# Opposite array quarters for the two heads of a pair in an RWKV-7 chunk recurrence

## The chip, the cores and the metric

The kernel runs on one core of one Trainium2 chip. The metric is device time in microseconds, the median of three runs. TensorE (PE in the profile) multiplies: a weight tile is loaded into its array of 128 rows by 128 columns, and the moving operand streams past it; a product that has only 64 rows (summed over) or only 64 columns (outputs) uses a half of the array, one with 64 of each a quarter, and one with 32 of each a sixteenth. VectorE (DVE), ScalarE (ACT) and GpSimd (POOL) work element by element, SyncE (SP) issues the DMAs. TensorE writes to PSUM banks (512 fp32 values in each of 128 partitions), the other engines move the results on.

## The reference

One layer of a streaming encoder over 256 tokens and 2048 features. The combined projection feeds two groups of heads; their outputs go through one output projection, and a squared-ReLU MLP follows.

```python
h = rms_norm(x, norm_mix); proj = h @ w_in
q_d, k_d, v_d, rw = split(proj)                   # 8 heads of differential attention | RWKV-7
a_out = diff_attention(...)                       # two softmax maps per head: p0 - lam * p1
rw = token_shift(rw, mu); r, kr, vr, lat_w, lat_a, lat_g = split(rw)
w_log  = -softplus(-(w0 + tanh(lat_w) @ w2)) - 0.5; decay = exp(-exp(w_log))
a_rate = sigmoid(a0 + lat_a @ a2);  g = sigmoid(lat_g) @ g2
kk = normalised(kr * k_k); k_mod = kr * (1 + (a_rate - 1) * k_a)
# 16 heads of 64 features, state S (64 x 64) per head, over 256 tokens:
S_t = S_(t-1) diag(w_t) + (S_(t-1) a_t) b_t^T + v_t k_t^T;  y_t = S_t r_t     # a = -kk, b = kk * a_rate
y = (group_norm(y) + bonus) * g
x = x + concat(a_out, y) @ w_out
x = x + square(relu(rms_norm(x) @ mlp_up)) @ mlp_down
```

## The kernel before

The four weight matrices are streamed in tiles of 256 x 512. Each is split exactly into two parts (`hi` by ACT, `lo` by DVE, `split`), and three products per 128 rows and token tile give the result (`gemm`; the products named `acc` in the profile). While the tiles of `w_in` and the first half of `w_out` go by, side work runs beside them: RWKV-7 in two halves of eight heads, then attention in two halves of four heads. A side task is a generator; each `yield dve, act, hop` declares what its next stage costs VectorE and ScalarE and how many weight tiles it waits, and `pump` lets a task go on while the credit of `BD` and `BA` (2.0 us each) per weight tile lasts.

All instructions are first taken down by `Recorder` (so every row of the profile has line 292), then put in order by `plan`: a list scheduler with costs for each instruction. Each engine takes the instruction that can start first, earlier ones before later; weight splits get a rank 120 places ahead (`SPL`). The chip executes each engine's list in that order. Side products share four PSUM banks (tags `sm` and `tr`), weight products have four more.

The recurrence works in chunks of 64 tokens, four per half. For each half of eight heads:

- `seg_kr` makes decay and rate through low-rank products (`lora_mm`): one with both parts of the weights under each other (128 rows), one with the small part of the latents (64 rows, `XL`).
- `seg_b` and `seg_r` write the decayed r, k, a and b into `AR` and `BK`, whose columns hold a chunk pair as [r|k even, a|b even, a|b odd, r|k odd]; the partitions hold the 64 features of two heads, of which the even one has partitions 0 to 63.
- `seg_a` multiplies `BK` and `AR` into the chunk matrices `Am` (64 rows, 128 columns, 128 elements a head; four heads of one row half, then four of the other), masks them, sends the block N of each through DRAM to one block a partition, inverts the diagonal 32-blocks there, and joins them by products of 32x32 (`TP`, `Rm`).
- `seg_c` runs the chunks in turn. The bank `XY` takes `Am` over V (rows of r|k, 128 columns) and the state product `AR` over `Sp`. Its a|b part goes to `X`, `Rm` over `X` gives U (`UV` holds V and U under each other), `tm` over `UV` gives the state (128 rows, 64 columns, heads of a pair in alternate column halves), and `Am` over U is added to the r|k part of `XY`, which becomes `Y`.

All eight heads of a chunk use the same row half in these products: `pk, pb = 64 * e, 64 - 64 * e` with `e = c % 2`. The attention (`seg_attn`) multiplies q and k of the two maps, which lie in the two row halves (64 rows), one map after the other.

After the side work of a half, `finish` lets what is left of its tasks go on, and the output projection multiplies y first and the attention's output second (`gemm([ys[1], as_[1]], ...)`).

## Time and profile before

| | us |
|---|---|
| three runs | 1237.98, 1239.23, 1240.45 (median 1239.23) |
| span of the profiled execution (first to last instruction) | 1236.8 |
| median of the runs over that span | 2.4 |
| PE busy | 1225.0 |
| DVE busy | 842.1 |
| ACT busy | 727.0 |
| POOL busy | 6.7 |
| mean granted TensorE clock | 0.999 |

The profile gives a span for its execution and no time of its own; what a run has around the span is taken from the difference to the median. Busy time of PE counts from the start of a product to the end of its last result, and products overlap; so a block of products is best read from its start to the start of the row behind it.

### The profile page before, as it was taken

To read this page: it belongs to the slowest core of one execution; us is meant where nothing else is said; L and a number is where in the kernel's file an instruction comes from. 1 tells how busy PE (TensorE), PEld (TensorE's weight loads), DVE (VectorE), ACT (ScalarE), POOL (GpSimd) and SP (SyncE) were. 2 spreads that over 40 slices of the span, in tenths; PEclk is the share of its full clock that TensorE was granted. 3 is DMA by queue.
4 is the path that set the end of the run, shared out by engine and by line. 5 is a ranking of instruction groups with operands and counts; after the bars stand their busy time and mean duration, and the time that the engine had idled before them with its cause. 6 is when DMAs were issued, how large, how long until landed. Compare 5 with 4: busy or idle time off the path is not lost.

```text
span 1236.8 us, 16428 instructions
## 1 busy us (share of the span) xinstructions
PE 1225.0 (99%) x6089; PEld 988.9 (80%) x6089; DVE 842.1 (68%) x1257; ACT 727.0 (59%) x1145; POOL 6.7 (1%) x28
## 2 busy tenths in 40 slices
PE   8999999999999999999999999999999999999998
PEld 6878887888778788878788787887887887888786
DVE  5578684697847776777747648658658558567754
ACT  6684455665567667977447447456457356357532
POOL 1000000000000000000000000000000000000000
PEclk9999999999999999999999999999999999999999
DMA  8745646256442645566565665665665665666564
GB/s 256 204 142 158 168 135 179 63 145 171 128 138 90 228 153 167 173 187 204 187 188 181 193 187 178 196 187 174 201 177 181 203 176 184 203 172 199 192 205 135
DMA packets 126560, 216.10 MB, mean 175 GB/s; under 512 B 21584, under 2 KB 24400, under 8 KB 126480
## 3 DMA queue, kind: packets, MB, share of 16 engines
q1 hardware_dynamic: 126480, 215.05, 57.5%
q8 instruction: 48, 0.79, 0.3%
q14 instruction: 32, 0.26, 0.1%
HBM read 211.09 MB, written 3.93 MB: 174 GB/s over the span
## 4 chain that ended last, share of the span: by engine, by line
PE 93%; ACT 3%; DVE 2%; DMA 1%; issue 1%; SPq 0%; ACTq 0%
PE acc L292 83%; PE sm L292 7%; PE tr L292 3%; ACT z L292 1%; DVE z L292 1%; ACT hi L292 1%; DMA x<-x 1%; DVE lo L292 0%; DMA TP<-Td 0%; ACT hT L292 0%; SPq L292 0%; ACT junk L292 0%; DVE hT L292 0%; DVE x L292 0%; DMA Td<-N 0%
## 5 line engine op out<-in xcount | busy, mean ns | idle before, releaser
L292 DVE TENSOR_TENSOR lo<-raw,hi 128x1024 fp32r<-128x1024 f32 (+2 forms) x393 | 474.2, 1210 | 307.0 <-ACT hi L292 303.3
L292 ACT CAST hi<-raw 128x1024 fp32r<-128x1024 f32 (+2 forms) x393 | 405.6, 1038 | 336.9 <-PE acc L292 316.6
L292 PE MATMUL acc<-hi,u 128*128 128x512 f32 x1024 | 324.0, 395 | 2.7 <-DVE z L292 2.7
L292 PE MATMUL acc<-hi,hT 128*128 128x512 f32 x1024 | 322.6, 395 | 0.0
L292 PE MATMUL acc<-hi,xT 128*128 128x512 f32 (+1 forms) x832 | 267.3, 395 | 1.2 <-ACT hi L292 1.2
L292 PEld LDWEIGHTS acc<-hi,u 128*128 128x128 f32 x1024 | 192.8, 188 | 50.5 <-issue 5.5
L292 PEld LDWEIGHTS acc<-hi,hT 128*128 128x128 f32 x1024 | 192.8, 188 | 45.2
L292 PE MATMUL acc<-lo,hT 128*128 128x512 f32 x512 | 202.1, 395 | 0.2 <-DVE lo L292 0.2
L292 PE MATMUL acc<-lo,u 128*128 128x512 f32 x512 | 202.0, 395 | 0.0
L292 PEld LDWEIGHTS acc<-hi,xT 128*128 128x128 f32 x832 | 153.4, 189 | 33.6 <-ACT hi L292 1.7
L292 PE MATMUL acc<-lo,xT 128*128 128x512 f32 (+1 forms) x416 | 163.4, 393 | 0.1
L292 ACT ACTIVATE z<-acc,rstd 32x128 f32<-32x128 f32 x256 | 91.9, 359 | 47.2 <-DVE z L292 27.3
L292 PEld LDWEIGHTS acc<-lo,hT 128*128 128x128 f32 x512 | 96.4, 188 | 23.1 <-DVE lo L292 0.6
L292 PEld LDWEIGHTS acc<-lo,u 128*128 128x128 f32 x512 | 96.4, 188 | 22.2
L292 DVE TENSOR_SCALAR z<-acc,rstd 32x128 f32<-32x128 f32 x256 | 90.2, 352 | 18.6 <-ACT z L292 14.9
L292 PEld LDWEIGHTS acc<-lo,xT 128*128 128x128 f32 x416 | 78.4, 189 | 16.0 <-DVE lo L292 1.0
L292 DVE TENSOR_TENSOR x<-x,acc 128x512 f32<-128x512 f32 x80 | 52.0, 680 | 5.6 <-PE acc L292 5.4
L292 PE MATMUL acc<-hi,y 128*128 128x512 f32 x128 | 42.7, 400 | 0.0
L292 PE MATMUL acc<-hi,a 128*128 128x512 f32 x128 | 42.1, 398 | 0.0
L292 ACT ACTIVATE uf<-uf 128x1024 f32<-128x1024 f32 x16 | 17.0, 1062 | 35.8 <-DVE uf L292 35.8
L292 PEld LDWEIGHTS acc<-hi,a 128*128 128x128 f32 x128 | 24.0, 188 | 5.9 <-issue 0.3
L292 PEld LDWEIGHTS acc<-hi,y 128*128 128x128 f32 x128 | 23.9, 189 | 5.5 <-issue 0.3
(228 smaller groups left out, 850.3 us busy)
## 6 DMA issues: line engine op xcount, KB each, us to landing
raw<-up SPq DMA_DIRECT2D x128, 512.0 KB, 3.8
raw<-down SPq DMA_DIRECT2D x128, 512.0 KB, 3.8
raw<-w_in SPq DMA_DIRECT2D x95, 512.0 KB, 3.7
raw<-w_out SPq DMA_DIRECT2D x32, 512.0 KB, 3.7
raw<-w_in SPq DMA_DIRECT2D x8, 288.0 KB, 2.9
x<-x SPq DMA_DIRECT2D x4, 512.0 KB, 6.5
out<-x SPq DMA_DIRECT2D x8, 256.0 KB, 3.4
x<-x SPq DMA_DIRECT2D x6, 256.0 KB, 7.9
```

The costliest lines, as they stand in the source:

```text
L292: op.fn(*op.args, **op.kw)
```

## The change

The two heads of a pair take opposite halves of the rows: with `first(c, q)` the r|k part of head q in chunk c stands at partition 64 * ((c + q) % 2). `AR` and `BK` are written by partition half with the columns ordered accordingly, `UV` and `Y` are copied in two column sets (`hcols`). In `seg_c` the state product comes first; then `Am` over V makes only the a|b part, with 64 columns, the two heads of a pair in opposite quarters of the array, as in the product with `Rm`. The output's r|k part is one product of `Am` over V and U (128 rows, 64 columns) behind the state. In `seg_a` and `seg_attn` the products of the two row halves are issued alternately into two banks, and the products of the inverses alternate between the two 64-row halves. In `lora_mm` the second product has 128 rows too, with zeros in the half that was left out (`XWL`, `XAL`); `lam_p` moves to a shared slot to make room for them. Declared costs of stages change with the copies. Comments and docstrings go. The core of the diff:

```diff
-    XW, XA, XL, G0, G0L, G1 = (cst.tile([P, T], F32R, name=n) for n in ("XW", "XA", "XL", "G0", "G0L", "G1"))
+    XW, XA, XWL, XAL, G0, G0L, G1 = (cst.tile([P, T], F32R, name=n) for n in ("XW", "XA", "XWL", "XAL", "G0", "G0L", "G1"))
+    nc.gpsimd.memset(XWL[64:128].bitcast(F32), 0.0)
+    nc.gpsimd.memset(XAL[0:64].bitcast(F32), 0.0)
...
-        nc.vector.tensor_sub(XL[0:64], lw, XW[0:64])
-        nc.vector.tensor_sub(XL[64:128], la, XA[64:128])
+        nc.vector.tensor_sub(XWL[0:64], lw, XW[0:64])
+        nc.vector.tensor_sub(XAL[64:128], la, XA[64:128])
...
-    def ab(X):
-        return X.rearrange("p (a x) -> p a x", x=256)[:, :, 64:192].rearrange("p a (e t) -> p a e t", e=2)
-    def kr_(X):
-        return X.rearrange("p (a g t) -> p a g t", g=4, t=64)[:, :, 0:4:3, :]
-    def g4(X):
-        return X.rearrange("p (a e) t -> p a e t", e=2)
-    def f4(X):
-        return X.rearrange("p f (c e t) -> p (f c) e t", c=2, e=2)
+    def rows(q):
+        return slice(64 * q, 64 * q + 64)
+    def quarter(X, q, inner):
+        v = X[rows(q)].rearrange("p (a g t) -> p a g t", g=4, t=64)
+        return v[:, :, 1:3, :] if inner else v[:, :, 0:4:3, :]
+    def ab(X, q):
+        return quarter(X, q, q == 0)
+    def kr_(X, q):
+        return quarter(X, q, q == 1)
+    def g4(X, q):
+        return X[rows(q)].rearrange("p (a e) t -> p a e t", e=2)
+    def f4(X, q):
+        return X[rows(q)].rearrange("p f (c e t) -> p (f c) e t", c=2, e=2)
+    def first(c, q):
+        return 64 * ((c + q) % 2)
+    def hcols(X, q):
+        return X.rearrange("p (f q i) -> p q f i", q=2, i=64)[:, q]
...
-    def lora_mm(Dx, X, rows, out, bias):
+    def lora_mm(Dx, X, XL, out, bias):
         for fp in range(2):
             b = bank("tr")
             for i in range(2):
                 f = 2 * fp + i
                 nc.tensor.matmul(b[:, i * T:(i + 1) * T], Dx[:, f * P:(f + 1) * P], X, start=True, stop=False)
-                nc.tensor.matmul(b[:, i * T:(i + 1) * T], Dx[rows, f * P:(f + 1) * P], XL[rows], start=False, stop=True)
+                nc.tensor.matmul(b[:, i * T:(i + 1) * T], Dx[:, f * P:(f + 1) * P], XL, start=False, stop=True)
...
-        yield 1.1, 0.0, 0
+        yield 2.2, 0.0, 0
         AR, BK = big("AR"), big("BK")
         H.AR, H.BK = AR, BK
-        nc.vector.tensor_mul(ab(AR), f4(kk), g4(G[:, :, 0:64]))
-        done()
-        yield 1.1, 0.0, 0
-        nc.vector.scalar_tensor_tensor(ab(BK), f4(tau), -0.5, g4(Gi), op0=ALU.mult, op1=ALU.mult)
-        done()
-        yield 1.1, 0.0, 0
-        nc.vector.tensor_mul(kr_(BK), f4(km), g4(Gi))
+        for q in range(2):
+            nc.vector.tensor_mul(ab(AR, q), f4(kk, q), g4(G[:, :, 0:64], q))
+        done()
+        yield 2.2, 0.0, 0
+        for q in range(2):
+            for e in range(2):
+                nc.vector.scalar_tensor_tensor(ab(BK, q)[:, :, e], f4(tau, q)[:, :, e], -0.5, g4(Gi, q)[:, :, e], op0=ALU.mult, op1=ALU.mult)
+        done()
+        yield 2.2, 0.0, 0
+        for q in range(2):
+            nc.vector.tensor_mul(kr_(BK, q), f4(km, q), g4(Gi, q))
...
-        yield 1.1, 0.0, 0
-        nc.vector.tensor_mul(kr_(H.AR), f4(r), g4(H.G[:, :, 1:]))
+        yield 2.2, 0.0, 0
+        for q in range(2):
+            nc.vector.tensor_mul(kr_(H.AR, q), f4(r, q), g4(H.G[:, :, 1:], q))
...
-            nc.scalar.copy(H.UV[0:64, 2 * t, :], b[0:64])
-            nc.scalar.copy(H.UV[64:128, 2 * t + 1, :], b[64:128])
+            for e in range(2):
+                for q in range(2):
+                    o = first(e, q)
+                    nc.scalar.copy(hcols(H.UV[o:o + 64, 2 * t + e, :], q), hcols(b[64 * e:64 * e + 64], q))
...
         for c in range(4):
-            e = c % 2
-            pb = 64 - 64 * e
             Am = ftile([P, 8, P], "Am")
             H.Am.append(Am)
-            for q in range(2):
-                yield 0.6, 0.0, 0
-                b = bank("sm")
-                rows = slice(64 * q, 64 * q + 64)
-                for i in range(4):
-                    cs = i * 512 + c * P
-                    nc.tensor.matmul(b[:, i * P:(i + 1) * P], H.BK[rows, cs:cs + P], H.AR[rows, cs:cs + P], start=True, stop=True)
-                nc.vector.tensor_mul(Am[:, 4 * q:4 * q + 4, :], b.rearrange("p (h t) -> p h t", h=4),
-                                     masks[:, e:e + 1, :].broadcast_to([P, 4, P]))
-            nc.sync.dma_start(Ndv[e, c // 2], Am[pb:pb + 64, :, pb:pb + 64])
+            yield 1.2, 0.0, 0
+            bs = [bank("sm") for _ in range(2)]
+            for i in range(4):
+                cs = i * 512 + c * P
+                for q in range(2):
+                    nc.tensor.matmul(bs[q][:, i * P:(i + 1) * P], H.BK[rows(q), cs:cs + P], H.AR[rows(q), cs:cs + P], start=True, stop=True)
+            for q, b in enumerate(bs):
+                e = (c + q) % 2
+                pb = 64 - first(c, q)
+                hs = slice(4 * q, 4 * q + 4)
+                nc.vector.tensor_mul(Am[:, hs, :], b.rearrange("p (h t) -> p h t", h=4), masks[:, e:e + 1, :].broadcast_to([P, 4, P]))
+                nc.sync.dma_start(Ndv[e, c // 2][:, hs], Am[pb:pb + 64, hs, pb:pb + 64])
...
+        yield 0.0, 1.0, 0
+        bvs = [bank("sm").rearrange("p (c h t) -> p c h t", c=2, h=8) for _ in range(2)]
+        for c2 in range(2):
+            for h in range(8):
+                for e in range(2):
+                    pb = 64 - 64 * e
+                    nc.tensor.matmul(bvs[e][pb + 32:pb + 64, c2, h, :], H.Am[2 * c2 + (e + h // 4) % 2][pb:pb + 32, h, pb + 32:pb + 64],
+                                     TP[pb:pb + 32, c2, h, :], start=True, stop=True)
         for e in range(2):
             pb = 64 - 64 * e
-            yield 0.0, 0.5, 0
-            b = bank("sm")
-            bv = b.rearrange("p (c h t) -> p c h t", c=2, h=8)
-            for c2 in range(2):
-                Am = H.Am[2 * c2 + e]
-                for h in range(8):
-                    nc.tensor.matmul(bv[pb + 32:pb + 64, c2, h, :], Am[pb:pb + 32, h, pb + 32:pb + 64], TP[pb:pb + 32, c2, h, :],
+            nc.scalar.copy(TP[pb + 32:pb + 64], bvs[e][pb + 32:pb + 64])
+        yield 0.0, 1.0, 1
+        bvs = [bank("sm").rearrange("p (c h t) -> p c h t", c=2, h=8) for _ in range(2)]
+        for c2 in range(2):
+            for h in range(8):
+                for e in range(2):
+                    pb = 64 - 64 * e
+                    nc.tensor.matmul(bvs[e][pb:pb + 32, c2, h, :], TP[pb + 32:pb + 64, c2, h, :], Rm[pb + 32:pb + 64, c2, h, 32:64],
                                      start=True, stop=True)
-            nc.scalar.copy(TP[pb + 32:pb + 64], bv[pb + 32:pb + 64])
-        yield 0.0, 0.0, 1
         for e in range(2):
             pb = 64 - 64 * e
-            yield 0.0, 0.5, 0
-            b = bank("sm")
-            bv = b.rearrange("p (c h t) -> p c h t", c=2, h=8)
-            for c2 in range(2):
-                for h in range(8):
-                    nc.tensor.matmul(bv[pb:pb + 32, c2, h, :], TP[pb + 32:pb + 64, c2, h, :], Rm[pb + 32:pb + 64, c2, h, 32:64],
-                                     start=True, stop=True)
-            nc.scalar.copy(Rm[pb:pb + 32, :, :, 32:64], bv[pb:pb + 32])
+            nc.scalar.copy(Rm[pb:pb + 32, :, :, 32:64], bvs[e][pb:pb + 32])
...
+        heads_ = [(f, q, slice(f * P + 64 * q, f * P + 64 * q + 64)) for f in range(4) for q in range(2)]
         for c in range(4):
-            e = c % 2
-            pk, pb = 64 * e, 64 - 64 * e
             Am = H.Am[c]
-            yield 0.0, 0.5, 1
+            pks = [first(c, q) for q in range(2)]
+            kr_rows, ab_rows = [slice(o, o + 64) for o in pks], [slice(64 - o, 128 - o) for o in pks]
+            yield 0.0, 0.6, 1
             XY = bank("sm")
-            if True:
-                for h in range(8):
-                    cs = slice(h * 64, h * 64 + 64)
-                    nc.tensor.matmul(XY[:, cs], Am[pk:pk + 64, hq(h), :], UV[pk:pk + 64, c, cs], start=(h == 0), stop=True,
-                                     skip_group_check=True)
             if c:
                 for f in range(4):
                     nc.tensor.matmul(XY[:, f * P:(f + 1) * P], H.AR[:, f * 512 + c * P:f * 512 + (c + 1) * P], Sp[:, f, :],
-                                     start=False, stop=True, skip_group_check=True)
+                                     start=(f == 0), stop=True, skip_group_check=True)
+            for f, q, cs in heads_:
+                nc.tensor.matmul(XY[ab_rows[q], cs], Am[kr_rows[q], 4 * q + f, ab_rows[q]], UV[kr_rows[q], c, cs],
+                                 start=(not c and f == 0), stop=True, skip_group_check=True)
             X = stile([P, 512], "X", 1)
-            nc.scalar.copy(X[pb:pb + 64], XY[pb:pb + 64])
-            yield 0.0, 0.5, 1
+            for q in range(2):
+                nc.scalar.copy(hcols(X[ab_rows[q]], q), hcols(XY[ab_rows[q]], q))
+            yield 0.0, 0.6, 1
             Ub = bank("sm")
-            for h in range(8):
-                cs = slice(h * 64, h * 64 + 64)
-                nc.tensor.matmul(Ub[pb:pb + 64, cs], H.Rm[pb:pb + 64, c // 2, hq(h), :], X[pb:pb + 64, cs], start=True, stop=True)
-            nc.scalar.copy(UV[pb:pb + 64, c, :], Ub[pb:pb + 64])
-            yield 0.7, 1.2, 1
+            for f, q, cs in heads_:
+                nc.tensor.matmul(Ub[ab_rows[q], cs], H.Rm[ab_rows[q], c // 2, 4 * q + f, :], X[ab_rows[q], cs], start=True, stop=True)
+            for q in range(2):
+                nc.scalar.copy(hcols(UV[ab_rows[q], c, :], q), hcols(Ub[ab_rows[q]], q))
+            yield 0.7, 1.3, 1
             if c < 3:
                 Sb = bank("sm")
-                for h in range(8):
-                    o = (h // 2) * P + 64 * (h % 2)
-                    nc.tensor.matmul(Sb[64 * (h % 2):64 * (h % 2) + 64, (h // 2) * 64:(h // 2) * 64 + 64],
-                                     H.tm[c][:, o:o + 64], UV[:, c, h * 64:h * 64 + 64], start=True, stop=True)
+                for f, q, cs in heads_:
+                    nc.tensor.matmul(Sb[rows(q), f * 64:f * 64 + 64], H.tm[c][:, cs], UV[:, c, cs], start=True, stop=True)
                 Sbv = Sb[:, :256].rearrange("p (f j) -> p f j", f=4)
                 gc = H.GC[:, :, c:c + 1].broadcast_to([P, 4, 64])
                 if c:
...
                     nc.gpsimd.memset(Sp, 0.0)
                 nc.scalar.copy(Sp[0:64, :, 0:64], S[0:64])
                 nc.scalar.copy(Sp[64:128, :, 64:128], S[64:128])
-            for h in range(8):
-                cs = slice(h * 64, h * 64 + 64)
-                nc.tensor.matmul(XY[pk:pk + 64, cs], Am[pb:pb + 64, hq(h), pk:pk + 64], UV[pb:pb + 64, c, cs], start=False, stop=True,
-                                 skip_group_check=True)
-            nc.scalar.copy(Y[pk:pk + 64, c // 2, :], XY[pk:pk + 64])
+            for f, q, cs in heads_:
+                nc.tensor.matmul(XY[kr_rows[q], cs], Am[:, 4 * q + f, kr_rows[q]], UV[:, c, cs], start=False, stop=True, skip_group_check=True)
+            for q in range(2):
+                o = 64 * (c % 2)
+                nc.scalar.copy(hcols(Y[o:o + 64, c // 2, :], q), hcols(XY[kr_rows[q]], q))
...
-                for m in range(2):
-                    rows = slice(64 * m, 64 * m + 64)
-                    b = bank("sm")
-                    bv = b[:, :2 * nk].rearrange("p (h k) -> p h k", h=2)
-                    for i in range(2):
-                        hd = 2 * hp + i
-                        nc.tensor.matmul(bv[:, i, :], H.q[rows, hd, qt * P:(qt + 1) * P], H.k[rows, hd, :nk], start=True, stop=True)
+                bvs = [bank("sm")[:, :2 * nk].rearrange("p (h k) -> p h k", h=2) for _ in range(2)]
+                for i in range(2):
+                    hd = 2 * hp + i
+                    for m in range(2):
+                        rows = slice(64 * m, 64 * m + 64)
+                        nc.tensor.matmul(bvs[m][:, i, :], H.q[rows, hd, qt * P:(qt + 1) * P], H.k[rows, hd, :nk], start=True, stop=True)
+                for m, bv in enumerate(bvs):
```

## Rows read from the trace of the kernel before

**Rows 1.** The page: busy us, share of the span and instructions of each engine.

```profile
PE 1225.0 (99%) x6089; PEld 988.9 (80%) x6089; DVE 842.1 (68%) x1257; ACT 727.0 (59%) x1145; POOL 6.7 (1%) x28
```

**Rows 2.** What PE waited for from 60 to 470 us: in total, times, longest.

```profile
PE sm L292 <- DMA TP<-Td: 0.5, 1, 0.5
```

**Rows 3.** Two stretches: length, then busy us of PE, PEld, DVE, ACT, POOL.

```profile
60.00:414.00 354.00, 353.38 (x2265) 286.00 (x2265) 257.19 (x455) 217.63 (x354) 0.84 (x2) 1.00 0.49 138
226.00:280.00 54.00, 54.00 (x366) 44.62 (x365) 48.59 (x72) 35.21 (x53) 0.53 (x1) 1.00 0.40 117
```

**Rows 4.** PE's timeline in chunks of the first half: start us, us, instruction.

```profile
210.28 1.14 PE L292 MATMUL sm<-X,Rm 64*64 64x64 f32 x16
211.36 0.50 PE L292 MATMUL acc<-lo,xT 128*128 128x512 f32 x1
213.18 0.69 PE L292 MATMUL sm<-UV,tmbk 128*64 128x64 f32 x16
213.79 1.14 PE L292 MATMUL sm<-UV,Am 64*64 64x64 f32 x16
214.87 0.38 PE L292 MATMUL tr<-con,hss 128*8 128x128 f32 x2
217.32 2.00 PE L292 MATMUL sm<-UV,Am 64*128 64x64 f32 x16
219.13 0.49 PE L292 MATMUL sm<-rb,spread 64*128 64x256 f32 x2
```

**Rows 5.** PE's timeline, chunk matrices of one chunk.

```profile
266.72 1.71 PE L292 MATMUL sm<-AR,BK 64*128 64x128 f32 x16
268.36 0.72 PE L292 MATMUL acc<-hi,xT 128*128 128x512 f32 x2
```

**Rows 6.** PE's timeline, attention scores in two stages.

```profile
308.95 0.72 PE L292 MATMUL sm<-k,q 64*128 64x128 f32 x8
309.60 0.73 PE L292 MATMUL acc<-hi,xT 128*128 128x512 f32 x2
...
319.12 1.13 PE L292 MATMUL sm<-k,q 64*128 64x256 f32 x4
320.18 0.50 PE L292 MATMUL acc<-hi,xT 128*128 128x512 f32 x1
```

**Rows 7.** PE's timeline, low-rank products of the decay, then gate products.

```profile
160.30 0.28 PE L292 MATMUL tr<-XW,DW 128*128 128x256 f32 x1
...
162.69 0.50 PE L292 MATMUL acc<-hi,xT 128*128 128x512 f32 x1
163.03 0.39 PE L292 MATMUL acc<-lo,xT 128*128 128x512 f32 x1
163.26 0.62 PE L292 MATMUL acc<-hi,xT 128*128 128x512 f32 x2
...
248.57 0.28 PE L292 MATMUL sm<-G,gp 128*128 128x256 f32 x1
248.69 0.28 PE L292 MATMUL sm<-G0L,gp 128*128 128x256 f32 x1
```

**Rows 8.** PE's timeline, a block of the inverses.

```profile
200.19 1.17 PE L292 MATMUL sm<-TP,Am 32*32 32x32 f32 x32 [0.48 <-DMA TP<-Td]
201.28 0.50 PE L292 MATMUL acc<-lo,xT 128*128 128x512 f32 x1
```

**Rows 9.** Groups by form, DVE and ACT: shapes, count, busy us, mean ns, idle.

```profile
L292 DVE TENSOR_TENSOR AR<-kk,G 128x1024 f32<-128x1024 f32 x2 | 2.4, 1224 | 0.1
...
L292 ACT COPY Sp<-S 64x256 f32<-64x256 f32 x12 | 4.8, 402 | 3.5 <-DVE S L292 3.3
L292 ACT COPY X<-sm 64x512 f32<-64x512 f32 x8 | 4.6, 579 | 3.6 <-PE sm L292 3.6
```

**Rows 10.** PE's timeline, last transposes of the attention and their first use.

```profile
468.52 1.03 PE L292 MATMUL tr<-con,ao 128*128 128x128 f32 x8
...
473.58 0.40 PE L292 MATMUL acc<-hi,a 128*128 128x512 f32 x1
```

More of the change, by code (lines that the diff above doesn't have):

```diff
@@ L586, in record @@
     nc.vector.tensor_scalar(sub8, pc("sub"), 0.8, None, op0=ALU.mult)
-    lam_p = stile([P, 2, 64], "lam", 1)
+    lam_p = ftile([P, 2, 64], "lam")
     nc.vector.tensor_mul(lam_p, pc("lq").rearrange("p (c d) -> p c d", c=2), pc("lk").rearrange("p (c d) -> p c d", c=2))
@@ L752, in seg_kr @@
         th = ftile([P, 4, T], "th")
-        lora_mm(DW, XW, slice(0, 64), th, [w0h[:, f0 + f:f0 + f + 1] for f in range(4)])
+        lora_mm(DW, XW, XWL, th, [w0h[:, f0 + f:f0 + f + 1] for f in range(4)])
         kr = ftile([P, 4, T], "kr")
@@ L787, in seg_kr @@
         tau = ftile([P, 4, T], "tau")
-        lora_mm(DA, XA, slice(64, 128), tau, [a0h[:, f0 + f:f0 + f + 1] for f in range(4)])
+        lora_mm(DA, XA, XAL, tau, [a0h[:, f0 + f:f0 + f + 1] for f in range(4)])
         yield 1.2, 1.3, 1
```

## Prediction

> **What bounds the kernel now.** I read the page's busy times first: TensorE (PE) is busy 1225.0 of a span of 1236.8 us, VectorE (DVE) 842.1, ScalarE (ACT) 727.0 [rows 1]. A busy share alone could hide waiting, so the next view was the waits of PE between 60 and 470 us, the stretch in which the recurrence and the attention run beside the weight products: PE waited once, for 0.5 us [rows 2]. In that stretch PE therefore goes from one product to the next, and a side product costs the kernel exactly the time by which it pushes the following weight product away. The third view is PE's timeline: the price of a block of side products is the start of the next row less its own start, not its "us" column, which counts the last product's tail as well. The windows say what else is near its limit: from 60 to 414 us DVE is busy 257.2 of 354 us and ACT 217.6, but from 226 to 280 us DVE is busy 48.6 of 54 [rows 3]. An fp32 product stands in the trace as two records (sixteen for the eight heads of a chunk) [rows 4]; blocks are counted in records here.
>
> **The change part by part, savings on PE first.** Eight chunks are run (two halves of heads, four chunks each).
>
> (a) The first product of a chunk, Am over UV, uses 64 rows and 128 columns for eight heads in one row half, all sixteen records behind one another: 1.81 us (217.32 to 219.13) [rows 4]. Afterwards it has 64 columns, and the heads of a pair alternate between opposite quarters. The trace has no such block. Lower bound of its price: the state product, sixteen records alternating between two column halves, 0.61 us (213.18 to 213.79). Upper bound: sixteen records of 64x64 in one quarter, the product with Rm, 1.08 us (210.28 to 211.36) [rows 4]. I take 0.61, since quarters that share neither rows nor columns are further apart than the halves that already overlap. Eight times 1.20 is 9.6 us (at 1.08: 5.8).
>
> (b) The product with Rm goes from one quarter to two opposite ones: 1.08 to 0.61, eight times 0.47, 3.8 us; nothing if the quarters do not overlap.
>
> (c) The second product of the output (64x64, 1.08 us, 213.79 to 214.87) becomes one over 128 rows with 64 columns, in alternating column halves. That is the shape of the state product, so 0.61 is shown: 3.8 us, and up to 4.6 because it follows the state product without a change of shape.
>
> The Trainium skill, page "TensorEngine Tiling (Array Packing)", Restrictions and Gotchas, Gotcha 1, says that different row tiles cannot access the same PSUM bank at once. In (a) and (b) the two heads use different row halves and write the same bank, though different partitions of it; by that rule the twins would take turns, and the sum would be 7.6 us smaller. The rows that overlap here are either one row tile (state product, one bank) or two row tiles with two banks (scores), so the trace does not decide it.
>
> (d) Chunk matrices: sixteen records per chunk, first one row half, then the other: 1.64 us (266.72 to 268.36) [rows 5]. Interleaved twins on two row halves are seen in the scores: eight records in 0.65 us (308.95 to 309.60) [rows 6]. Of that some 0.2 us is the change of shape at entry and exit (a weight product behind a 64-row block takes 0.34 us, 162.69 to 163.03, against 0.23 for the next [rows 7]), so sixteen cost about 1.10. That saves 0.54 for a block that stands alone (4.3 in all), less where two chunks follow each other and overlap at the seam already; with two separate 0.65 it would be 2.7. I take 3.6.
>
> (e) Inverses: blocks of 32 records of 32x32 at 1.09 us (200.19 to 201.28) [rows 8], eight of them, 8.7 us. They become four blocks of 64 with twins in different row groups. Full overlap saves 4.4, none saves 0.3 (fewer changes of shape). By the ratio of (b), 0.61 to 1.08, it is 3.8, which I take.
>
> (f) The low-rank products of decay and rate: eight in 2.39 us (160.30 to 162.69) [rows 7], four such blocks, 9.6 us. Every second one has 64 rows, so the shape changes at each. With zeros in the other rows all have 128, like the gate products that start 0.12 us apart (248.57 to 248.69) [rows 7]: about 1.0 us a block. 5.6 us, and 0.4 for four exits without a change: 6.0 (5.0 to 6.1).
>
> (g) Scores: where both banks were free the twins overlap already (0.65 us for eight); a block in which one bank came late takes 1.06 us for four records (319.12 to 320.18) [rows 6] and is paid twice. Only such stages gain: 1.0 us, between 0 and 2.
>
> (h) Fewer changes of shape in the recurrence, because the first product now stands behind the product with Sp and the output behind the state product: six to eight changes of some 0.11 us, 0.9 (0 to 1.8).
>
> Sum: 9.6 + 3.8 + 3.8 + 3.6 + 3.8 + 6.0 + 1.0 + 0.9 = 32.5 us. With every bound at its bad end 17.6, at its good end 36.6.
>
> **What it adds.** On DVE three products of 128x1024 at 1.22 us become two each of 64 partitions; time goes by the elements of a partition, so each costs twice 1.22; the one with the scalar becomes four of half length, about 2.6 us. That is 5.1 us a half, 10.2 in all. On ACT 32 copies of 64x512 at 0.58 us become 64 of 64x256, at 0.40 by the copies of Sp [rows 9]: 7.0 us. SP issues eight more DMAs for the blocks N (half the size each); weight loads stand behind them in its queue, but they run tiles ahead. All of this is hidden by PE so long as the side work keeps pace with the weight tiles. From 60 to 414 us PE would need about 354 - 31 = 323 us, and DVE 257 + 10 = 267: covered on average. Between 226 and 280 us it is not: the 5.1 us of the second half fall there, PE shortens by two chunks and four matrices (some 6 us), and DVE would need 53.7 us of 48. The order written out beforehand gives the weight splits precedence, so some 6 us of side work slide back rather than PE stopping. What is late next is the attention of the second head group: its output is transposed at 468.52 and first multiplied at 473.58 [rows 10], a margin of 5 us. The chunk's chain also grows, by the first product (0.61) that now waits for Sp and by three split copies (0.22 each), 1.3 us a chunk; weight products cover it. For all this I take back 3 us (0 to 15).
>
> Net 29.5. The profiled span of 1236.8 becomes 1207.3; the median of the runs, 1239.23, lies 2.4 above that span, so the prediction is **1210 us**.
>
> **Rivals.** *Twins in one bank take turns.* This is the rule on banks above as a mechanism of this kernel: in (a) 1.08 instead of 0.61, in (b) nothing. It costs 7.6 us: 1217. For it: no overlapping pair of row halves in the trace shares a bank. Against: the state product's column halves share one and overlap.
>
> *The side work becomes the bound.* DVE's slack between 60 and 414 us falls from 97 to 56 us, and in its full stretches to nothing; if the two joins (before each half of the output projection) each wait for an attention that is 5 to 10 us late beyond the margin, 10 to 17 us are lost in place of 3: 1217 to 1224. For it: the full stretch and the margin of 5 us [rows 3, 10]. Against: the 56 us that are left.
>
> *Slower than before.* A paired stage takes two of the four side banks before it starts. There are twenty such stages (four of matrices, two of inverses, four of scores in each half). PE executes in the written order, so a second bank that is not free holds up the weight products behind it. It decides from 1.5 us a stage (29.5 / 20); at 2 us the kernel takes 1250. Against: PE waits 0.5 us in all now, and the order is planned with the banks in it.
>
> *No new overlap at all.* If interleaving brings nothing, only the shapes gain: (a) 5.8, (c) 3.8, (e) 0.3, (f) 6.0, less 3: 1226.
>
> **How the numbers follow.** Forecast 0.62 (its own range 1203 to 1216), bank rule 0.15, side work 0.15, no overlap 0.03, blocked stages 0.05. About 0.2% (2.5 us) is what a measurement of this kernel can tell from no change. Only blocked stages reach the other side, 0.04 slower and 0.01 within; side work adds 0.01 within: faster 0.94, same 0.02, slower 0.04. The range runs from 1202 (36 us gained, nothing given back) to 1225, which takes in the bank rule and the side work and leaves out most of the last two.
>
> **What would show it.** PE's timeline: sixteen records of the first product, of the product with Rm and of the output in 0.6 us each; matrices 1.1; inverses 64 records in 1.1 to 1.7; low-rank products 0.12 apart. Starts of twins only some ns apart would confirm (a) and (b), an even 0.06 the bank rule. PE's waits between 60 and 470 us should stay below 4 us; waits on weight splits or on the attention's output would show the side work, waits of side products on ACT or DVE the blocked stages. What would make it wrong most: a written order so different that PE waits where nothing waits now.

## The result and the profile after

The changed kernel takes 1224.55 us (median of four runs, 1224.13 to 1227.26) against 1238.61 for the kernel before on the same chip: ratio 0.9893, 95% interval 0.9881 to 0.9906. It is 14 us faster; 29.5 were forecast (1210 us), so less than half of the gain came, and the time lies at the upper end of the range (1202 to 1225). The profiled span is 1222.3 us.

The page, busy us of each engine, answers to [rows 1]:

```profile
PE 1208.6 (99%) x6089; PEld 973.5 (80%) x6089; DVE 848.4 (69%) x1269; ACT 734.9 (60%) x1179; POOL 7.3 (1%) x30
```

PE's timeline (start us, us, instruction), answers to [rows 4], [rows 6] and [rows 8]:

```profile
203.23 1.19 PE L292 MATMUL sm<-TP,Am 32*32 32x32 f32 x32
...
206.76 1.01 PE L292 MATMUL sm<-Rm,TP 32*32 32x32 f32 x27
207.71 0.50 PE L292 MATMUL acc<-lo,xT 128*128 128x512 f32 x1
208.14 1.36 PE L292 MATMUL sm<-Rm,TP 32*32 32x32 f32 x32
209.43 0.47 PE L292 MATMUL sm<-X,Rm 64*64 64x64 f32 x2
209.83 0.79 PE L292 MATMUL acc<-hi,xT 128*128 128x512 f32 x1
210.55 1.11 PE L292 MATMUL sm<-X,Rm 64*64 64x64 f32 x14
...
212.84 1.12 PE L292 MATMUL sm<-UV,tmbk 128*64 128x64 f32 x16
213.75 1.07 PE L292 MATMUL sm<-UV,Am 128*64 128x64 f32 x14
...
217.40 0.68 PE L292 MATMUL sm<-UV,Am 64*64 64x64 f32 x16
218.01 0.50 PE L292 MATMUL sm<-rb,spread 64*128 64x256 f32 x2
...
220.46 0.69 PE L292 MATMUL sm<-UV,tmbk 128*64 128x64 f32 x16
220.98 0.63 PE L292 MATMUL sm<-UV,Am 128*64 128x64 f32 x14
221.93 0.50 PE L292 MATMUL acc<-hi,xT 128*128 128x512 f32 x1 [0.33 <-ACT pvr L292]
...
317.14 1.13 PE L292 MATMUL sm<-k,q 64*128 64x256 f32 x4
318.19 0.50 PE L292 MATMUL acc<-hi,xT 128*128 128x512 f32 x1
...
322.80 1.13 PE L292 MATMUL sm<-k,q 64*128 64x256 f32 x4
323.86 0.50 PE L292 MATMUL acc<-hi,xT 128*128 128x512 f32 x1
```

Three things are to be seen. The first product's sixteen records take 0.61 us (217.40 to 218.01): opposite quarters do overlap. The paired stages often do not run as pairs: two records of the product with Rm run alone, then a weight product, then fourteen; an inverse block stands as 32 records by themselves; the scores of the two maps, four records each, are 5.66 us apart. And between the weight products (`acc`) that start at 209.83 and 221.93 there is no other: a pause of 12.1 us. It ends when ACT has evacuated `pvr`, the second half's last projection. The kernel before had a pause of 7.8 us; the weight products on either side of it:

```profile
212.85 0.40 PE L292 MATMUL acc<-lo,xT 128*128 128x512 f32 x1
...
220.62 0.72 PE L292 MATMUL acc<-hi,xT 128*128 128x512 f32 x2
```

The windows from 200 to 225 us, before and after (length, busy us of PE, PEld, DVE, ACT, POOL, then the granted clock):

```profile
200.00:225.00 25.00, 24.81 (x294) 19.91 (x294) 6.49 (x9) 13.12 (x22) 0.00 (x0) 1.00 0.34 107
```

```profile
200.00:225.00 25.00, 23.79 (x312) 19.13 (x312) 8.18 (x11) 16.33 (x33) 0.00 (x0) 0.86 0.39 108
```

From 208.97 to 215.80 us, for 6.8 us, TensorE's clock is at its lower level, 1.2 GHz; it did not fall there before. The fall begins just ahead of the pause, at the end of the inverses' blocks: 96 records of 32x32 and one weight product from 205.72 to 209.43.

PE's time by kind of product, from each record's start to the next one's, summed over the trace, so that waits behind a record and stretches at the lower clock are in it (the last two columns are kernels of the experiments):

```
us                        before  after  forecast  grouped  grouped + freed load
(a) first product, (c) output  23.84  11.69   10.4    11.45     9.64
(b) product with Rm             8.58   7.88    4.8     7.48     5.29
(d) chunk matrices             12.44  11.33    8.8     9.36     8.47
(e) inverses                    8.96   8.68    5.2     6.58     4.68
(f) low-rank products           9.64   4.59    3.6     4.58     3.91
(g) scores                      8.56  10.55    7.6     6.64     7.04
sum                            72.02  54.72   40.4    46.09    39.03
```

So TensorE saved 17.3 us in these kinds, not 31.6 ((a) to (g) of the forecast), and some 3 us of that went back: the product with Sp takes 0.8 us more than before, the other side products 2.2.

### The profile page after: what moved, and what is told of

It reads as the page before. It is cut to its first block, busy times and chain, and to the rows that moved or that the text cites. A ratio compares the mean times of both kernels' runs of the same rounds, so it can differ in the third digit from the quotient of the medians.

```text
span 1222.3 us, 16497 instructions
## 1 busy us (share of the span) xinstructions
PE 1208.6 (99%) x6089; PEld 973.5 (80%) x6089; DVE 848.4 (69%) x1269; ACT 734.9 (60%) x1179; POOL 7.3 (1%) x30
## 2 busy tenths in 40 slices
DMA packets 126689, 216.11 MB, mean 177 GB/s; under 512 B 21712, under 2 KB 24528, under 8 KB 126608
## 4 chain that ended last, share of the span: by engine, by line
PE 89%; ACT 6%; DVE 2%; issue 1%; DMA 1%; SPq 0%; ACTq 0%
PE acc L292 82%; PE sm L292 5%; PE tr L292 3%; ACT hi L292 1%; ACT z L292 1%; DVE z L292 1%; DMA x<-x 1%; DVE lo L292 1%; ACT UV L292 0%; ACT junk L292 0%; ACT hT L292 0%; SPq L292 0%; DVE hT L292 0%; ACT L292 0%; DVE x L292 0%
## 5 line engine op out<-in xcount | busy, mean ns | idle before, releaser
L292 PEld LDWEIGHTS acc<-hi,y 128*128 128x128 f32 x128 | 23.8, 188 | 5.8 <-issue 0.3
```

What stands on the lines that cost most here:

```text
L292: op.fn(*op.args, **op.kw)
```

## The experiments

Times are medians; each ratio is to the kernel before on the same chip, with its 95% interval.

**Twins kept together (T1), the transfers' queue (T2), VectorE's work (T3).** The order is written by `plan`, which takes whichever product can start first. X, the inverse's operands and the score banks become ready in parts, so it issues one twin before the other.

```diff
...
+    for g in groups.values():          # the products of one paired stage
+        ext = set().union(*(o.deps for o in g)) - set(g)
+        want = list(dict.fromkeys(n for o in g for n in o.tiles))
+        for o in g:
+            o.deps |= ext              # ready together
+            o.want = want              # claim their banks together
...
```

> Every paired stage (first product, product with Rm, state, output, chunk matrices, the two inverse stages, scores) is kept together in the written order: its products become ready together and claim their banks together. Nothing else changes. Theory T1 (the twins were pulled apart by the written order, since their operands and banks become ready at different moments, so that the forecast sum of 32.5 us came out as about 19): the inverse stages overlap their twins (8.7 to 5 us), the product with Rm falls from 7.9 to about 5, scores from 10.6 to about 7, chunk matrices from 11.3 to about 9; the kernel takes 1209 to 1215 us, 10 to 15 below the changed kernel. Theory T3 (the added VectorE and ScalarE work gave the gain back): TensorE's blocks shorten as above, but waits take their place, and the time stays within 3 us of 1224.5. Theory T4 (a stage that needs two banks at once blocks the written order): slower than 1224.5, with TensorE waiting for VectorE or ScalarE.

Measured 1218.52 (0.9844, 0.9831 to 0.9857): 6.0 us better, not 10 to 15. The stages shorten (table, 8.6 us in sum): scores and chunk matrices as T1 says, the inverses to 6.6 us and not 5, the product with Rm to 7.5 and not 5, since its two blocks in the pause take 3.5, at the lower clock or with a wait behind them. T4 falls. The edit joins the twins' operands and their banks at once, so it does not tell which of the two had parted them. But the pause grows:

```profile
202.93 0.39 PE L307 MATMUL acc<-hi,xT 128*128 128x512 f32 x1
...
220.95 0.50 PE L307 MATMUL acc<-hi,xT 128*128 128x512 f32 x1 [0.32 <-ACT pvr L307]
```

TensorE is there 7 us earlier and resumes 1 us earlier: 18.0 us of pause.

```diff
-                nc.sync.dma_start(Ndv[e, c // 2][:, hs], Am[pb:pb + 64, hs, pb:pb + 64])
+                nc.gpsimd.dma_start(Ndv[e, c // 2][:, hs], Am[pb:pb + 64, hs, pb:pb + 64])
```

> The eight transfers a half that take the chunk blocks N to DRAM are issued from GpSimd's queue instead of SyncE's, where they stand between weight loads that wait for buffers. Nothing else changes. Theory T2 (SyncE's in-order queue delays the inverse by some 8 to 10 us a half, the recurrence and the attention are late, bulk products run out of slots near 206 to 222 us and the clock falls to half for 6.8 us): the inverse of the first half starts near 141 us instead of 149, TensorE keeps 2.4 GHz through 206 to 222 us, and the kernel takes 1219 to 1222 us. T1 alone (the delay costs nothing, since weight products cover it): within 1.5 us of 1224.5, the clock falls as before or elsewhere.

Measured 1227.35 (0.9908, 0.9895 to 0.9921): nothing gained. All eight transfers are issued by 129 us instead of 140, and the load of N that follows them still stands at 143.94 in SyncE's queue. T2 as stated falls; what places that load stayed open.

> Both edits: paired stages kept together, and the transfers of N on GpSimd's queue. If T1 and T2 both hold, their gains add: 1205 to 1211 us. If T1 alone: 1209 to 1215, like the grouped kernel. If T2 alone: 1219 to 1222. If T3 (VectorE and ScalarE work is the bound): not below 1221.

Measured 1219.15 (0.9842, 0.9828 to 0.9856), like the grouped kernel.

```diff
+            nc.vector.tensor_mul(ab(AR, q), f4(kk, q), g4(G[:, :, 0:64], q))    # and two more, each a second time
```

> The six half-width VectorE products that the change made out of three (k and a, k and r columns of AR and BK) are executed twice each, with the same values: about 14.6 us more VectorE work in all, half of it in each half of the heads. Theory T3 (the added VectorE and ScalarE work gave the gain back): the kernel takes 5 to 15 us longer than the changed one, 1230 to 1240 us, with TensorE waiting for VectorE or for the late attention. T1 and T2: covered by TensorE, within 2 us of 1224.5.

Measured 1244.85 (1.0053, 1.0039 to 1.0068): 20 us lost, more than the work itself. Of the theories only T3 allows that, though the other way round nothing happens:

```diff
-        for q in range(2):
+        for q in range(1):             # in AR and BK; the second head's half is zero
...
```

> The changed kernel without the VectorE work that it added: of AR and BK only the first head's half is computed (four products a half of heads, as many and as long as before), the second head's half is set to zero by GpSimd, so the recurrence of every second head works on zeros. TensorE executes the same products. T5 with T3 (VectorE is full between 60 and 125 us, so the 5 us added there delay the first half's recurrence, and the end of the pause, one for one): the pause ends 4 to 6 us earlier and the kernel takes 1217 to 1221 us. T1 alone: within 2 us of 1224.5. The added work as the whole cause: 1214 us or less.

Measured 1224.99 (0.9893, 0.9877 to 0.9909): unchanged. In its trace the first half's inverse starts at 149.23 us, as in the changed kernel (149.36), and the pause is longer, 19.8 us, with the clock down for 17.1. So the added VectorE work is not what holds the inverse back; since the pause came out differently, this run does not price that work by itself (the run with N's load freed, below, does it better).

**What the pause waits for (T5), and the clock (T6).** As I read the program, from about 143 us on all 18 working tiles are taken. The evacuation into `pvr` needs one, and gets it when the first half's second chunk is through; with two projections complete in PSUM and neither evacuated, weight products stop. (In the changed kernel with one tile more, below, that evacuation starts at 209.39 us instead of 221.19.) If so, a shorter recurrence ends the pause:

```diff
-        for t in range(31, 0, -1):
+        for t in range(31, 0 if hh else 15, -1):
```

> The grouped kernel with 16 of the 31 steps of the first half's forward substitution on VectorE left out (that half's inverse is incomplete, so its output is not the reference's). TensorE executes the same products; the recurrence's chain of the first half gets shorter by 15 to 20 us. T5: the pause of 18 us falls below 5, the clock stays up there, and the kernel takes 1204 to 1211 us. If the first half's chain is not what sets the pause: within 2 us of 1218.5.

Measured 1209.50 (0.9770, 0.9757 to 0.9783), 9.0 us better than the grouped kernel. The longest stretch without a weight product near 200 us is 3.6, and the clock stays up. The first half's recurrence is what the pause waits for. The steps left out are also 10.4 us less work for VectorE; the freed load of N (below) takes no work from it and gains as much.

```diff
-        t_r = task(seg_r(H, hh, project(3072 + 512 * hh, 512, "pr")), 2, (t_b,))
+        t_r = task(seg_r(H, hh, project(3072 + 512 * hh, 512, "prx" if hh else "pr")), 2, (t_b,))
```

> The changed kernel; only the projected r of the second head half is held in one of the 8 large tiles (one is unused there) and not in one of the 18 working tiles, so one more working tile is free from about 143 us on. Theory T5 (the first half's recurrence is the critical path to 221 us: all 18 working tiles are taken, and the evacuation of the next projection waits until the second chunk frees one; weight products then pause, 212.8 to 220.6 us before, 209.8 to 221.9 after, 202.9 to 220.9 with grouped twins, so TensorE's savings up to there are waited away and the clock falls): the pause of 12.1 us shrinks below 4, the clock stays at 2.4 GHz there, and the kernel takes 1212 to 1219 us. T3 in its plain form (VectorE's and ScalarE's total work is the bound) and T1 alone: within 2 us of 1224.5.

> Both: paired stages kept together and the projected r of the second half in a large tile. T5: the pause of 18 us shrinks below 5, and the gain of grouping shows in full: 1202 to 1210 us, 8 to 16 below the grouped kernel. Without T5: within 2 us of 1218.5.

> The kernel before, with the projected r of the second half in a large tile; the control for the two above. T5: before has a pause of 7.8 us in weight products, but TensorE fills it with side products and its clock does not fall, so little is to be had: 0 to 4 us faster, 1234.5 to 1238.5. If the free tile is worth as much here as in the changed kernel (6 us or more), T5 does not explain the missing gain of the change.

Measured: grouped kernel 1212.33 (0.9788, 0.9774 to 0.9801), 6.2 better, pause 12.3 instead of 18.0, not below 5. But the changed kernel 1232.70 (0.9953, 0.9940 to 0.9965), 8 worse, although no pause is left near 200 us, and the kernel before 1248.37 (1.0084, 1.0070 to 1.0098), 10 worse; all three forecasts missed. In these two the clock ran at its lower level for 10.2 us (and 3.4 later) and for 20.5 us. In the kernel before this fits the loss; in the changed one stretches of over 6 us without weight products appear near 380 and 413 us, whose cause was not followed. A tile more is no cure by itself.

```diff
...
+            if not hh and c < 2:
+                filler(3)              # products of zeros, behind each stage of the first half's chain
...
```

> The changed kernel with products of zeros (64 columns of zero weights over 512 columns of data, 0.21 us each, into a bank that nobody reads) between the stages of the first half's inverse and of its first two chunks, 28 in all, 6 us if none hides in an idle moment. Theory T6 (the fall of TensorE's clock to half for 6.8 us in the pause comes of little work on TensorE there, and costs half of it): the granted clock stays at 2.4 GHz through 200 to 222 us, the recurrence's blocks there run at full speed, and the kernel takes 1219 to 1223 us. If the clock costs nothing because the pause is set by the side chain's other engines: 1224.5 to 1228, the fillers' own price on top.

> The same fillers in the kernel with grouped stages and the extra free tile (1212.3, half clock for 6.8 us). T6: 1208 to 1211 us. Without T6: 1212 to 1216.

Measured 1228.19 (0.9924, 0.9911 to 0.9936) and 1215.33 (0.9818, 0.9804 to 0.9831). But the fillers did not run where they were meant to. They need nothing from the chain, so `plan` put all 28 ahead of it (count, ns of one, first and last start):

```profile
L292 PE MATMUL sm<-xT,zw x28: 387/394/473, 7.4 to 174.2; 128*64 128x512 f32 x28
```

In the second kernel the last one starts at 173.9 us. So T6 was not tested. What the two runs do show: 6.7 us more of PE's timeline, spent ahead of the pause, cost 3.6 and 3.0 us. In both the pause is gone (2.7 and 2.9 us without a weight product at most near 200 us), and the clock fell for 3.4 us only in the first, not at all there in the second. What a fall costs is better read from executions of one program: the changed kernel with N's load freed (below) took 1217.34 us at a mean granted clock of 0.999 and 1222.76 at 0.994.

**One part alone on the kernel before.** Only the 128-row low-rank products:

> The kernel before with one edit of the change alone, the low-rank products with 128 rows (part f). All of them run before 165 us. By the plain sum, TensorE saves 5 us and so does the kernel: 1232.5 to 1234.5. Theory T5 (what TensorE saves before the pause is waited away in the pause, because the first half's recurrence ends no earlier): the pause grows from 7.8 to 10 to 13 us, and the kernel gains at most 2 us: 1236 or more; with a fall of the clock in the pause it may even lose.

Measured 1230.95 (0.9950, 0.9937 to 0.9962): 7 us, all of the plain sum and more. The pause did not grow (7.0 us); it moved forward as a whole, from 212.85 to 205.65, and the load of N with it, from 134.39 to 129.97. So what TensorE saves early is not always waited away. In the changed kernel N's load did not move forward, and that pointed back to it:

SyncE's queue in the changed kernel (start us, us, instruction):

```profile
118.84 0.65 SPq L292 DMA_DIRECT2D Nd<-Am  x1
...
131.43 0.57 SPq L292 DMA_DIRECT2D Nd<-Am  x1
133.79 0.37 SPq L292 DMA_DIRECT2D raw<-w_in  x1
134.21 0.57 SPq L292 DMA_DIRECT2D Nd<-Am  x1
136.58 0.37 SPq L292 DMA_DIRECT2D raw<-w_in  x1
137.00 0.57 SPq L292 DMA_DIRECT2D Nd<-Am  x1
139.37 0.37 SPq L292 DMA_DIRECT2D raw<-w_in  x1
139.79 0.57 SPq L292 DMA_DIRECT2D Nd<-Am  x1
142.16 0.35 SPq L292 DMA_DIRECT2D lwa<-lora_wa  x1
144.99 0.95 SPq L292 DMA_DIRECT2D N<-Nd  x2
```

and in the kernel before:

```profile
121.13 1.83 SPq L292 DMA_DIRECT2D Nd<-Am  x2
...
130.66 0.58 SPq L292 DMA_DIRECT2D Nd<-Am  x1
133.04 0.37 SPq L292 DMA_DIRECT2D raw<-w_in  x1
134.39 0.95 SPq L292 DMA_DIRECT2D N<-Nd  x2
```

A weight load stands between any two of the last transfers, and the load of N behind them all, 10.6 us later than before. The place is written by `plan`: it takes a DRAM tile as one region (`if ap.space == PSUM or ap.space == DRAM: p0, p1, f0, f1 = 0, 127, 0, 1 << 30`), so each transfer into `Nd` counts as waiting until the one before has landed.

**The load of N freed (T8).**

```diff
                 for (q0, q1, g0, g1, w, o) in last.setdefault(t.name, []):
+                    if w and write and ap.space == DRAM:
+                        continue
```

> The changed kernel; when the order is written, transfers that write the same DRAM tile no longer count as waiting for one another (they write different blocks). Only the written order changes. Theory T8 (the order counts each of the transfers of N as waiting until the one before it has landed, some 2.8 us each; four such steps a half before, eight after, so the load of N stands about 11 us later in SyncE's queue, behind four more weight loads, wherever the eight are issued from, and the first half's recurrence with it): N is loaded near 131 to 135 us instead of 145, the pause of weight products ends 6 to 10 us earlier than 221.9, the clock does not fall or falls less, and the kernel takes 1213 to 1219 us. If the place of that load is not what delays the first half: within 2 us of 1224.5.

> The same edit of the order in the kernel with grouped stages (1218.5, pause of 18 us to 220.9). T8: the pause ends 6 to 10 us earlier: 1206 to 1212 us, about what the kernel with the shortened substitution takes (1209.5). Without T8: within 2 us of 1218.5.

> The same edit of the order in the kernel before; the control. T8: only four such steps were counted there, N's load moves forward by some 4 to 5 us, and there was no fall of the clock to undo: 0 to 4 us faster than before, 1234 to 1238. If it gains as much as the changed kernel does, the change has not lost its gain there.

Measured: changed kernel 1220.68 (0.9853, 0.9833 to 0.9873), 3.9 better; grouped kernel **1205.69** (0.9735, 0.9721 to 0.9749), 12.8 better; kernel before 1239.41 (1.0007, 0.9998 to 1.0016), no gain. N is loaded at 131.35, 129.67 and 129.54 us. In the control the load comes 4.9 us earlier, the pause moves forward by 4.4 us and stays 7.8 long, and nothing is gained: only the changed kernels had something to win back. The edit lets `plan` write the whole order anew, so more than N's load moves; that the gain comes through the first half's recurrence is borne out by the shortened substitution, which gained 9.0 us with the load left at 143.45. Of the grouped kernel with the freed load, the page, the same window, and PE's timeline:

```profile
PE 1192.4 (99%) x6089; PEld 961.2 (80%) x6089; DVE 850.2 (71%) x1269; ACT 732.4 (61%) x1179; POOL 7.3 (1%) x30
```

```profile
200.00:225.00 25.00, 24.75 (x266) 19.60 (x265) 17.30 (x21) 20.23 (x41) 0.53 (x1) 1.00 0.30 86
```

```profile
192.47 1.20 PE L309 MATMUL sm<-TP,Am 32*32 32x32 f32 x64
...
198.54 0.68 PE L309 MATMUL sm<-X,Rm 64*64 64x64 f32 x16
...
212.86 0.39 PE L309 MATMUL acc<-hi,xT 128*128 128x512 f32 x1
...
216.05 0.48 PE L309 MATMUL acc<-hi,xT 128*128 128x512 f32 x1
...
260.27 1.16 PE L309 MATMUL sm<-AR,BK 64*128 64x128 f32 x16
261.37 0.50 PE L309 MATMUL acc<-hi,xT 128*128 128x512 f32 x1
...
305.63 1.13 PE L309 MATMUL sm<-k,q 64*128 64x256 f32 x8
306.69 0.51 PE L309 MATMUL acc<-hi,xT 128*128 128x512 f32 x1
```

The clock stays at 1.00, the pause is 3.2 us, an inverse block is 64 records together, the product with Rm sixteen, and eight records of the scores now cost what four did. The ungrouped kernel has no pause left near 200 us either, but gained less: in its profiled execution (1222.22 us) the clock fell for 3.4 us at 198.82 and for 10.2 at 338.77, each time in or just behind inverses' blocks that stood as in the changed kernel (194.38 to 197.85 and 335.64 to 339.88); its fastest execution, at a mean granted clock of 0.999, took 1217.34, inside T8's forecast. The cause of the falls was not tried.

> The same edit of the order in the changed kernel without the added VectorE work (the second head's half of AR and BK set to zero by GpSimd, so every second head's recurrence works on zeros). Without the edit, leaving out that work changed nothing (1225.0). If the added 5 us a half delayed the first half too, and were only hidden behind the transfers of N: N is loaded 4 to 7 us earlier than with the edit alone, and the kernel takes 2 to 6 us less than it. If the added work is covered altogether: within 2 us of it.

Measured 1220.36 (0.9856, 0.9834 to 0.9878): N is loaded 3.9 us earlier (127.42), and the time stays. The executions spread with the clock, from 1218.66 at 1.000 to 1227.08 at 0.992, so 2 us could hide in them; but at the same 0.999 this kernel took 1218.77 and the one with the added work 1217.34. With no pause left near 200 us, no gain of an earlier first half is seen.

> The kernel with grouped stages and the freed load of N (1205.7, the pause down to 3.2 us), in which the added VectorE products are executed twice, 14.6 us more VectorE work, as in the run of the changed kernel that lost 20 us by it. If that work costs because it delays the first half's recurrence, which the changed kernel could no longer bear (T8), and there is room again: 1206 to 1212 us, the pause back to 5 to 12 us. If VectorE's total work is the bound in itself (T3): 1217 us or more.

Measured 1216.96 (0.9826, 0.9813 to 0.9840), 11.3 us lost to 14.6 us of work: above T8's forecast and at the edge of T3's. N is loaded at 139.63, 10.0 us later, and the pause is back, 11.5 us (207.75 to 219.22), as T8 says, with the clock up and TensorE waiting:

```profile
200.00:225.00 25.00, 21.32 (x331) 16.93 (x331) 11.66 (x14) 18.25 (x39) 0.00 (x0) 1.00 0.39 112
```

So VectorE's work ahead of N does delay the first half's recurrence. Half of the added work lies in the second half, behind the pause; how the 11.3 us divide between the two, and how much of them is VectorE's total work (T3), this run does not tell. The 10 us that the change itself added found cover, 15 more did not.

> The same kernel (1205.7) with the projected r of the second half in a large tile, so that one more working tile is free from about 143 us on. If the pause still costs something: 1202 to 1205 us. If it is gone as a cost: within 2 us of 1205.7.

Measured 1205.73 (0.9736, 0.9723 to 0.9749): the 3.2 us of pause that are left cost nothing.

## Why the prediction was wrong

The sum on TensorE was right for twins that run as twins. In the grouped kernel with the freed load, (a) to (g) save 33.0 us by the table, against 31.6 forecast for them, and the kernel gains 32.3 (1238.0 to 1205.7). What failed are two steps of the text. The sign that it named did not show it: PE's waits from 60 to 470 us are 3.0 us in sum, below the 4 us allowed, because TensorE spends the pause on side products, in part at the lower clock.

*"Interleaved" twins, steps (b), (d), (e) and (g).* I priced them as if issuing them alternately in the program meant executing them alternately. They save 0.7, 1.1, 0.3 and -2.0 us instead of 3.8, 3.6, 3.8 and 1.0, because the written order takes each twin when its own operand or bank is ready. For (b) that is less than half of it: its first two chunks, in the pause, take 1.4 and 1.5 us at the lower clock or with a wait behind them, and the other six 0.8 on average, five of them with two records ahead of fourteen, instead of 0.61. (c) is 2.0 us over its forecast, 1.5 of it in the same two chunks. In (g) the pairs that overlapped before [rows 6] were pulled apart. Keeping them together gives 8.6 us of PE's time, but only 6.0 to the kernel, because the pause grows to 18.0 us by the next step.

*"SP issues eight more DMAs ... they run tiles ahead", taken at nothing.* I asked what stands behind them for the weights, and not for N. N is loaded at 144.99 us instead of 134.39, the first half's inverse starts at 149.36 instead of 141.29, its recurrence holds the working tiles longer, and TensorE, being faster, meets the pause earlier: 12.1 us instead of 7.8. Freeing that load is worth 3.9 us in the changed kernel and 12.8 with the twins together; the two losses hide each other, and only both cures together give the forecast. The clock, down for 6.8 us in the changed kernel, stood in no term of the sum; it did not fall near 200 us in the kernel with both cures.

Right were: (a), 10.4 against 9.6, by overlapping quarters; (f), 5.1 against 6.0, and (f) alone on the kernel before gains even 7.0; the DVE and ACT work as covered (10.4 and 8.5 us by the sum of the instructions' durations, against 10.2 and 7.0), with (from the doubled work) less room than I gave it. (h) did not come: with both cures the product with Sp takes 0.8 us more than before and the state product 0.5 less.

The rival of the banks falls. The two heads of (a) use different row halves and write one bank, at 0.61 us for sixteen records. The Trainium skill, page "TensorEngine Tiling (Array Packing)", Restrictions and Gotchas, Gotcha 1, says that different row tiles cannot access the same PSUM bank at once; here the measurement decides against it, at least for quarters that write different partitions of the bank. The rival of blocked stages came closest to what failed in kind, though not in its effect: by the rows the stages did not hold PE up until both twins could go, they went one twin at a time. Whether bank or operand parted them is not shown.

Open are what makes the clock fall, near 200 us and at 338.77 us in the ungrouped kernel with N's load freed, and how the loss by a tile more in the kernel before divides between the clock and the order.

## What to carry to other kernels

A pair that should overlap must be one unit for whatever writes the order; otherwise each half runs when its own operand arrives. A product added to fill a gap needs a dependency that holds it there; without one it is executed ahead of the gap. Before counting a saving on the bound engine, find the next place where that engine runs ahead of its buffers and what frees them: a saving is kept only if that chain moves forward too, and a transfer that is cheap in itself can move the chain by its place in a queue. When two cures each give little, try them together.

## What was not expected of the hardware

Products on opposite quarters into one bank start only some 7 ns apart, pair after pair at 58 ns, at 2.4 GHz (first product, 217.51 to 217.86 us); at 1.2 GHz pairs of the product with Rm come every 107 ns (210.82 to 211.25). So the sixteen records of the state product took 0.91 us at the lower clock (212.84 to 213.75) and 0.52 a chunk later (220.46 to 220.98).

The clock fell in stretches in which PE was busy all along by the profile (23.8 of 25 us in the changed kernel), and it stayed up in one with a pause of 11.5 us, in which PE was busy 21.3 of 25 us (the doubled work). Neither the pause nor the profile's busy time tells the two apart. In the changed kernel it fell at the end of inverses' blocks with one weight product among 96 records of 32x32. In the kernel before, where weight products stand between these blocks, and in the grouped kernel with the freed load, where two blocks of 64 records stand 1.8 us apart, it did not fall there. This is what stood ahead of the falls, not a cause that was tried, and it does not cover all: in the kernel before with the freed load the clock fell for 3.4 us at 216.11, behind the first product.
